# One buffer for both halves of a split weight, and matmul operands at whole multiples of 64 bytes from each other

## The chip, the cores and the metric

The kernel runs on one core of one Trainium2 chip. The metric is the device time of one execution in microseconds (us). Memory addresses below are byte offsets within a partition of the on-chip memory (SBUF), as the built programs have them.

## The reference

One layer of a decoder trunk, in float32, on x of 512 positions by 1024 channels:

```python
h = rms_norm(x, g_pre_mix)
z = h @ w_in                    # columns: u, v, q, six k/v, gates, xr, rg, mg
y_a = gmlp_mixer(gelu(u), gelu(v), ...)     # causal 128-position chunks
y_b = nsa_mixer(q, k.., v.., nsa_g, ...)    # 16 heads: compressed, selected, window
y_c = rglru_mixer(xr, rg, ...)  # conv of width 4, gates r and i by x @ w_a, x @ w_x, linear scan
gates = sigmoid(mg)             # one for each branch
merged = gates[0] * (y_a @ w_br_a) + gates[1] * (y_b @ w_br_b) + gates[2] * (y_c @ w_br_c)
x = x + rms_norm(merged @ w_o, g_post_mix)
f_gate, f_up = split(rms_norm(x, g_pre_ffn) @ w_ffn_in)
return x + rms_norm((silu(f_gate) * f_up) @ w_ffn_out, g_post_ffn)
```

## The kernel before

Every large product is done in three matmuls. A weight tile of 128 x 1024 comes in as `raw`; ACT writes its rounded high half `hi` (L119) and DVE the rest, `lo` = raw - hi (L124), both 128 x 1024. The activations are split the same way (`hh` and `hl` are the halves of the normalized input). `passes` (L236) then runs, for each of eight 128-row pieces of the contraction, hi times xh, hi times xl and lo times xh, each a matmul of 128 x 128 weights with 512 columns: 24 matmuls for one unit. Of each matmul the weights are the stationary operand, which is loaded while the matmul before still streams its moving operand.

The stages, in order: the v half of the projection (L538, to about 50 us); units of L236 with the recurrent branch between them (L464: six matmuls a piece, with the block weights `wabh`, `wabl` as stationary and the halves `ch`, `cl` of the convolved tile as moving operand); attention from 383 to 648 us, where units of L236 alternate with scores (L850), transposes (L875) and values (L888: `ph`, `pl` moving, `V` stationary); the output projection (L1067); the first layer of the feed-forward part in 256-column matmuls (L1169, and L1303 on pairs of weight tiles combined as in Strassen's scheme, where `a22h` and `a22l` are one of the combined operands); its second layer (L1439, 512 columns). L766 is the other 256-column stage, at 350 us.

The order of work around this is written as generators that yield between matmuls; a scheduler in the build places the instructions of each engine by what they wait for and by when a pool gives its buffer. `unit` (L231) takes the next weight and has three loaded ahead. Tiles live in pools; a pool's tiles lie behind one another at fixed addresses, so a pool's start follows from the sizes of the pools before it: `const`, `mid` (rows, and the small attention statistics `pcst` and `ast`), `stage` (raw), `merge`, `wts` (hi and lo, three buffers each), `big`, then one pool per phase. `warm` is a constant of one column, 4 bytes, at the start.

The distance spoken of below is the address of a matmul's moving operand minus that of the stationary operand of the next matmul. Weight and activation pieces are 512 and 2048 bytes long, so within one pair of tiles the distance modulo 512 is the same for all pieces.

Of the kernel before, what the change touches and what calls it, by code (L numbers as in the profile page):

```python
# [22 lines left out]
F32 = mybir.dt.float32  # L23
F32R = mybir.dt.float32r
# [26 lines left out]
def hybrid_block(ctx: ExitStack, tc: tile.TileContext, A, out):  # L51
# [3 lines left out]
    const = ctx.enter_context(tc.tile_pool(name="const", bufs=1))  # L55

    mid = ctx.enter_context(tc.tile_pool(name="mid", bufs=1))
    stage = ctx.enter_context(tc.tile_pool(name="stage", bufs=2))
    merge = ctx.enter_context(tc.tile_pool(name="merge", bufs=1))
    wts = ctx.enter_context(tc.tile_pool(name="wts", bufs=2))  # L60
# [17 lines left out]
    def next_phase(i):  # L78
        if phase[0]:
            phase[0].__exit__(None, None, None)  # L80
        if i == 2:
            early.__exit__(None, None, None)
        phase[0] = tc.tile_pool(name=f"phase{i}", bufs=1, reuse_waits="tile")
        pool = phase[0].__enter__()
        for t in PHASES[i]:
            phase_pool[t] = (pool, PHASES[i][t])

    phase_pool = {}

    cnt = [0]  # L90

    def nm(s):
        cnt[0] += 1
        return f"{s}_{cnt[0]}"
# [4 lines left out]

    def row(name, dt=F32, tag="row"):  # L100
        return mid.tile([128, S], dt, tag=tag, name=nm(name), bufs={"row": 6, "q32": 2, "tg": 2}[tag])

    def bank(tag):
        return psum[1].tile([128, S], F32, tag=tag, name=nm(tag), bufs=psum[2][tag])
# [78 lines left out]
    def wload(upto):  # L183
        while wnext[0] < min(upto, wlimit[0]):
            i = wnext[0]
            ap, tag = wlist[i]
            if isinstance(ap, tuple):
                hi = wts.tile([128, 1024], F32R, tag="hi", name=nm("hi"), bufs=3)
                lo = wts.tile([128, 1024], F32R, tag="lo", name=nm("lo"), bufs=3)
                fo["prep"](*ap, hi, lo)  # L190
                wready[i] = (hi, lo)
                wnext[0] += 1
                continue
            raw = stage.tile([128, 1024], F32, tag="raw", name=nm("raw"), bufs=2)
            parts = [slice(0, 512), slice(512, 1024)] if i == 0 else [slice(0, 1024)]
            for n, p in enumerate(parts):
                (SC if i == n == 0 else SY).dma_start(raw[:, p], ap[:, p])
                if i == 0:
                    x_in(n + 1)
            if tag == "gate":  # L200

                hi = lo = wts.tile([128, 1024], F32R, tag="hi", name=nm("hi"), bufs=3)
                SC.activation(hi, raw, AF.Copy)
                r, h = (t.rearrange("p (k m) -> p k m", m=128)[:, :, 64:] for t in (raw, hi))
                V.tensor_sub(h, r, f32(h))
                wready[i] = (hi, lo)
                wnext[0] += 1
                continue
            if tag:
                u = slab("u", F32R, tag, (2, 1024))  # L210
                hi, lo = u[:, 0], u[:, 1]
            else:
                hi = wts.tile([128, 1024], F32R, tag="hi", name=nm("hi"), bufs=3)
                lo = wts.tile([128, 1024], F32R, tag="lo", name=nm("lo"), bufs=3)
            todo = [(raw[:, p], hi[:, p], lo[:, p], V) for p in parts]
            if i == 0:
                wfirst.extend(todo)
            else:
                split(*todo[0])
            wready[i] = (hi, lo)  # L220
            wnext[0] += 1
# [33 lines left out]
    def x_in(k):  # L255
        SY.dma_start(xt[k], A["xT"][:, k, :])
# [4 lines left out]
    wload(1)  # L261
    ones = const0([128, 128], "ones")
    V.memset(ones, 1.0)
    warm = const.tile([128, 1], F32, name="warm")
    V.memset(warm, 0.0)
    SC.activation(warm, warm, AF.Exp)
    ident = const.tile([128, 128], F32, name="ident")
# [58 lines left out]
    hh, hl = Pair("hh", F32R, "h"), Pair("hl", F32R, "h")  # L326
# [454 lines left out]
    def cmp_attn(g):  # L781
        if g == 0:
            yb["y"] = Pair("yb", tag="yb")
        ps = bank("tr")
        pv = ps.rearrange("p (a h n) -> p a h n", a=4, h=4)
        for a in range(4):
            for p in range(2):
                PE.matmul(ps[:, a * 128 + p * 64:a * 128 + p * 64 + 64],  # L788
                          at[g]["q32"][p][:, a * 128:(a + 1) * 128], kcb[:, g, :], start=True, stop=True)
        P = row("pc").rearrange("p (a h n) -> p a h n", a=4, h=4)  # L790
        P3 = P.rearrange("p a h n -> p (a h) n")
        st = mid.tile([128, 2, 4, 4], F32, tag="pcst", name=nm("pcst"), bufs=2)
        s0 = st[:, 0].rearrange("p a h -> p (a h)")
        for h in range(4):
            V.scalar_tensor_tensor(P[:, :, h, :], pv[:, :, h, :], 0.125, cmask, op0=OP.mult, op1=OP.add)
        yield
        V.tensor_reduce(s0, P3, axis=mybir.AxisListType.X, op=OP.max)
        V.tensor_tensor(P3, P3, s0[:, :, None].to_broadcast([128, 16, 32]), op=OP.subtract)
        Pf = P.rearrange("p a h n -> p (a h n)")
        SC.activation(Pf, Pf, AF.Exp)  # L800
        yield
        V.tensor_reduce(s0, P3, axis=mybir.AxisListType.X, op=OP.add)
        V.reciprocal(s0, s0)
        V.tensor_mul(st[:, 0], st[:, 0], gates[:, :, 12 * g:12 * g + 12:3])
        V.tensor_mul(P3, P3, s0[:, :, None].to_broadcast([128, 16, 32]))
        yield
        pt = bank("tr")
        for a in range(4):
            PE.transpose(pt[:, a * 128:(a + 1) * 128], P[:, a].rearrange("p h n -> p (h n)"), ident)

        PT = [row("pct", F32R) for _ in range(2)]
        for p in range(2):
            own, other = slice(64 * p, 64 * p + 64), slice(64 - 64 * p, 128 - 64 * p)
            SC.activation(PT[p][own], pt[own], AF.Copy)
            V.tensor_sub(PT[p][other], pt[own], f32(PT[p][own]))
        yield
        gs = slice(128 * g, 128 * g + 128)
        for p in range(2):
            po = bank("tr")
            PE.matmul(po, vch[:, gs], PT[p], start=True, stop=False)  # L820
            PE.matmul(po, vcl[:, gs], PT[p], start=False, stop=True)
            SC.activation(yb["y"][2 * g + p], po, AF.Copy)
            yield

    class Unit:
# [14 lines left out]
        def scores(self, j):  # L840
            g, a, n, brs = self.g, self.a, self.n, self.brs
            w = len(brs)
            if j == 0:
                self.T = slab("P", tag="P")
                self.st = mid.tile([128, 3, 4, w], F32, tag="ast", name=nm("ast"), bufs=3)
            st, K = self.st, at[g]["k"]
            ps = bank("sc")
            lhs = at[g]["q"][:, j, a * 128:(a + 1) * 128]
            for i in range(2):
                PE.matmul(ps[:, :w * n].rearrange("p (b n) -> p b n", b=w), lhs, K[:, i, brs[0]:brs[-1] + 1, :n],  # L850
                          start=(i == 0), stop=(i == 1))
            for b, br in enumerate(brs):
                t = self.part(j, br)
                V.tensor_tensor_reduce(out=t, in0=ps[:, b * n:b * n + n], in1=mask[0][:, S - n:], scale=-0.125,  # L854
                                       scalar=3.0e38, op0=OP.add, op1=OP.min, accum_out=st[:, 0, j, b:b + 1])
                SC.activation(t, t, AF.Exp, scale=-1.0, bias=st[:, 0, j, b:b + 1],  # L856
                              accum_out=st[:, 1, j, b:b + 1])
            if j == 3:
                V.reciprocal(st[:, 2], st[:, 1])
                for b, br in enumerate(brs):  # L860
                    V.tensor_mul(st[:, 2, :, b], st[:, 2, :, b], gates[:, a, 12 * g + 1 + br:12 * g + 12:3])

                own = 0 if w == 2 else 2
                for i in range(own):
                    t = self.part(i, brs[0])
                    SC.activation(t, t, AF.Copy, scale=st[:, 2, i, 0:1])
                for b, br in enumerate(brs):
                    o = b * n
                    t = self.T[:, own:4, o:o + n]
                    V.tensor_tensor(t, t, st[:, 2, own:4, b:b + 1].to_broadcast([128, 4 - own, n]), op=OP.mult)  # L870
# [333 lines left out]
    def first_weights():  # L1204

        ff["raw"] = [slab("rawp", tag="w2", shape=(2, 1024))]
        pair_load(HEAD)
        for _ in range(9):
            yield
        w = [tuple(wts.tile([128, 1024], F32R, tag=t, name=nm(t), bufs=3) for t in ("hi", "lo")) for _ in range(3)]  # L1210
        ff["ring"] = w
        ff["prep"] = pair_prep(HEAD)
        for _ in range(4):
            next(ff["prep"])
            yield
# [514 lines left out]
```

## Time and profile before

| what | value |
|---|---|
| median of 3 runs | 1115.99 us (1115.6 to 1116.36) |
| profiled execution | 1115.29 us, its span 1113.6 us |
| granted TensorE clock, mean | 0.998 |
| TensorE (PE) busy | 1103.9 us, 99%, 6152 matmuls |
| weight loads (PEld) busy | 954.8 us, 86% |
| DVE, ACT, POOL busy | 827.7, 625.7, 46.2 us |
| read from DRAM | 111.89 MB, 102 GB/s over the span |

The profiled execution is 0.7 us under the median. In the profile's rows "L236 PE MATMUL mm<-hl,hi" names the line, the output, and behind the arrow the moving and the stationary operand; "idle before" is the time in which the engine stood still ahead of such instructions, and the arrow behind it names what ended it. A matmul's duration reaches from its start to its modelled end and overlaps the next one's; the distance of two starts is what it costs in a row of matmuls.

### The profile page before, as it was taken

The numbers are of one execution on the slowest core, as the hardware profiler recorded it, in microseconds if no ns is written. First come the engines' busy times: TensorE is split into PE (matmuls) and PEld (weight loads), VectorE is DVE, ScalarE is ACT, GpSimd is POOL, SyncE is SP. The second block draws the span as 40 slices with busy tenths as digits, with TensorE's granted clock in tenths as the row PEclk, the third lists the DMA queues.
The fourth block names the chain that finished last, engine by engine and source line by source line (L and its number), as shares of the span: only waits on it lengthen the run. The fifth ranks groups of instructions, "written<-read, shape, count | busy, mean of one in ns | idle before, by whom it ended". The sixth has DMA issues, their size and how long they took to land.

```text
span 1113.6 us, 15969 instructions
## 1 busy us (share of the span) xinstructions
PE 1103.9 (99%) x6152; PEld 954.8 (86%) x6152; DVE 827.7 (74%) x1453; ACT 625.7 (56%) x1120; POOL 46.2 (4%) x59
## 2 busy tenths in 40 slices
PE   9999999999999999999999999999999999999997
PEld 8888778888888888888878888888999999998885
DVE  6966967262575899998998853567988787879665
ACT  6756674232344676776776632435655655567552
POOL 1000202100000000000000000000000000022200
PEclk9999999999999999999999999999999999999999
DMA  8332325323222211112112163421233332378902
GB/s 310 114 95 76 103 93 192 108 89 98 90 81 77 77 58 38 57 30 79 45 40 75 54 230 95 129 99 38 77 114 115 114 107 84 133 192 218 186 29 94
DMA packets 34653, 115.02 MB, mean 103 GB/s; under 512 B 3409, under 2 KB 3697, under 8 KB 33425
## 3 DMA queue, kind: packets, MB, share of 16 engines
q1 hardware_dynamic: 27200, 93.78, 25.5%
q0 software_dynamic: 5216, 11.18, 5.1%
q10 hardware_dynamic: 2160, 9.04, 2.2%
q8 instruction: 48, 0.79, 0.3%
q14 instruction: 29, 0.23, 0.1%
HBM read 111.89 MB, written 2.10 MB: 102 GB/s over the span
## 4 chain that ended last, share of the span: by engine, by line
PE 92%; DVE 4%; ACT 2%; DMA 1%; issue 0%; DVEq 0%; ACTq 0%
PE mm L236 39%; PE mm L1303 18%; PE mm L1439 6%; PE mm L538 4%; PE mm L1067 4%; PE o L888 4%; PE sc L850 3%; PE tr L875 3%; PE tr L1439 3%; PE mm L766 2%; PE tr L682 1%; DVE lo L124 1%; PE mm L1169 1%; PE tr L464 1%; PE tr L598 1%; PE tr L788 1%
## 5 line engine op out<-in xcount | busy, mean ns | idle before, releaser
L119 ACT ACTIVATE hi<-raw 128x1024 fp32r<-128x1024 f32 (+1 forms) x108 | 113.4, 1050 | 156.0 <-PE mm L236 77.1
L236 PE MATMUL mm<-hh,hi 128*128 128x512 f32 x504 | 199.9, 397 | 0.0
L236 PE MATMUL mm<-hh,lo 128*128 128x512 f32 x504 | 197.5, 392 | 0.2 <-DVE lo L124 0.2
L236 PE MATMUL mm<-hl,hi 128*128 128x512 f32 x504 | 197.2, 391 | 0.0
L124 DVE TENSOR_TENSOR lo<-raw,hi 128x1024 fp32r<-128x1024 f32 (+1 forms) x108 | 131.6, 1219 | 80.1 <-ACT hi L119 73.0
L236 PEld LDWEIGHTS mm<-hh,lo 128*128 128x128 f32 x504 | 94.7, 188 | 20.1 <-DVE lo L124 0.5
L236 PEld LDWEIGHTS mm<-hh,hi 128*128 128x128 f32 x504 | 94.7, 188 | 18.7 <-ACT hi L119 0.4
L236 PEld LDWEIGHTS mm<-hl,hi 128*128 128x128 f32 x504 | 94.8, 188 | 18.5 <-issue 0.2
L856 ACT ACTIVATE P<-P,ast 128x128 f32<-128x128 f32 (+3 forms) x128 | 70.6, 554 | 23.2 <-DVE ast L854 22.6
L854 DVE CUSTOM_DVE_ANT_0 P<-sc,mask 128x128 f32<-128x128 f32 (+3 forms) x128 | 57.9, 484 | 8.2 <-PE sc L850 7.3
L119 ACT ACTIVATE ph<-tr 128x512 fp32r<-128x512 f32 x80 | 46.9, 591 | 29.3 <-PE tr L875 28.4
L124 DVE TENSOR_TENSOR pl<-tr,ph 128x512 fp32r<-128x512 f32 x80 | 54.4, 685 | 5.0 <-ACT ph L119 3.0
L1303 PE MATMUL mm<-t,hi 128*128 128x256 f32 x288 | 53.3, 283 | 0.0
L1390 POOL DMA_DIRECT2D bs<-in_w_fo x16 | 19.3, 1212 | 792.0 <-DVE lo L124 792.0
L850 PE MATMUL sc<-K,q 128*128 128x512 f32 (+2 forms) x192 | 50.9, 367 | 0.0
L1439 PE MATMUL mm<-hi,u 128*128 128x512 f32 x160 | 50.3, 390 | 0.0
L875 PE MATMUL tr<-ident,P 128*128 128x128 f32 x320 | 48.7, 273 | 0.0
L875 PEld LDWEIGHTS tr<-ident,P 128*128 128x128 f32 x320 | 39.1, 140 | 9.8 <-DVE pl L124 0.9
L124 DVE TENSOR_TENSOR lo<-bs,hi 128x1024 fp32r<-128x1024 f32 x28 | 34.1, 1221 | 14.6 <-ACT hi L119 14.6
L1303 PEld LDWEIGHTS mm<-t,hi 128*128 128x128 f32 x288 | 44.8, 192 | 0.0
L1303 PE MATMUL mm<-fh,hi 128*128 128x256 f32 x144 | 41.0, 285 | 0.0
L1303 PE MATMUL mm<-fh,lo 128*128 128x256 f32 x144 | 40.7, 283 | 0.0
(384 smaller groups left out, 2760.0 us busy)
## 6 DMA issues: line engine op xcount, KB each, us to landing
raw<-in_w_in SPq DMA_DIRECT2D x64, 512.0 KB, 3.6
rawp<-in_w_fi SPq DMA_DIRECT2D x20, 1024.0 KB, 4.9
raw<-in_w_br SPq DMA_DIRECT2D x24, 512.0 KB, 3.6
bs<-in_w_fo POOLq DMA_DIRECT2D x20, 512.0 KB, 6.8
w<-in_cw ACTq DMA_DIRECT2D x4, 1024.0 KB, 6.2
raw<-in_w_o SPq DMA_DIRECT2D x8, 512.0 KB, 3.6
bs<-in_w_fo SPq DMA_DIRECT2D x8, 512.0 KB, 7.4
raw<-in_w_v SPq DMA_DIRECT2D x7, 512.0 KB, 5.2
```

Of the source, the lines that this page charges most:

```text
L119: res["hi"] = SC.activation(hi, src, AF.Copy)
L124: res["lo"] = V.tensor_sub(lo, src, f32(hi))
L236: res["mm"] = PE.matmul(ps[:m, n0:n1], w[:, k * 128:k * 128 + m], x[k][:, n0:n1], start=(t == 0), stop=(t == 3 * NK - 1))
L538: res["mm"] = PE.matmul(b[c], x[k][:, c * 128:(c + 1) * 128], w[:, kk * 512:kk * 512 + 512], start=(k == 0 and t == 0), stop=(k == NK - 1 ...
L850: PE.matmul(ps[:, :w * n].rearrange("p (b n) -> p b n", b=w), lhs, K[:, i, brs[0]:brs[-1] + 1, :n], start=(i == 0), stop=(i == 1))
L854: V.tensor_tensor_reduce(out=t, in0=ps[:, b * n:b * n + n], in1=mask[0][:, S - n:], scale=-0.125, scalar=3.0e38, op0=OP.add, op1=OP.min, a ...
L856: SC.activation(t, t, AF.Exp, scale=-1.0, bias=st[:, 0, j, b:b + 1], accum_out=st[:, 1, j, b:b + 1])
L875: PE.transpose(pt[:, j * 128:(j + 1) * 128], self.part(j, br)[:, kt * 128:(kt + 1) * 128], ident)
L888: PE.matmul(po, VV[:, kt, g % 2, br].rearrange("p i d -> p (i d)"), x, start=(br == 0 and kt == 0 and t == 0), stop=(br == 1 and kt == a a ...
L1067: res["mm"] = PE.matmul(b[c, f], x[k][:, q], w[:, fs], start=(k == 0 and t == 0), stop=(k == NK - 1 and t == 2))
L1303: res["mm"] = PE.matmul(ps, w[:, k * 128:k * 128 + 128], x[:, k], start=(start and k == t == 0), stop=(k == 3 and t == 2), skip_group_chec ...
L1439: PE.matmul(ps, a, b, start=id(ps) not in begun, stop=i == len(ops) - 1, skip_group_check=True)
```

## The change

A function `wpair` gives both halves of a weight as two slices of one tile of 2080 columns with three buffers. In every second tile the halves begin 16 columns (64 bytes) later. The column halves of the gate unit take the first slice of such a tile. The small statistics `pcst` and `ast` move from the pool `mid` to the phase's pool, `warm` becomes 17 columns long (64 bytes more), and the third phase's pool begins with an unused tile of 256 bytes, `gap`. In names after, `hl` stands for such a weight tile too (as in `mm<-hh,hl`), whichever half is used.

```diff
+        if i == 2:
+            pool.tile([128, 64], F32, name="gap", bufs=1)
...
+    wturn = [0]
...
+    def wpair():
+        o = 16 * (wturn[0] % 2)
+        wturn[0] += 1
+        w = wts.tile([128, 2080], F32R, tag="hl", name=nm("hl"), bufs=3)
+        return w[:, o:o + 1024], w[:, o + 1024:o + 2048]
...
-                hi = wts.tile([128, 1024], F32R, tag="hi", name=nm("hi"), bufs=3)
-                lo = wts.tile([128, 1024], F32R, tag="lo", name=nm("lo"), bufs=3)
+                hi, lo = wpair()
...
-                hi = lo = wts.tile([128, 1024], F32R, tag="hi", name=nm("hi"), bufs=3)
+                hi = lo = wpair()[0]
...
-    warm = const.tile([128, 1], F32, name="warm")
+    warm = const.tile([128, 17], F32, name="warm")[:, 0:1]
...
-        st = mid.tile([128, 2, 4, 4], F32, tag="pcst", name=nm("pcst"), bufs=2)
+        st = phase_pool["q"][0].tile([128, 2, 4, 4], F32, tag="pcst", name=nm("pcst"), bufs=2)
...
-                self.st = mid.tile([128, 3, 4, w], F32, tag="ast", name=nm("ast"), bufs=3)
+                self.st = phase_pool["q"][0].tile([128, 3, 4, w], F32, tag="ast", name=nm("ast"), bufs=3)
...
-        w = [tuple(wts.tile([128, 1024], F32R, tag=t, name=nm(t), bufs=3) for t in ("hi", "lo")) for _ in range(3)]
+        w = [wpair() for _ in range(3)]
```

What it makes of the addresses, modulo 512 bytes:

| tiles | before | after |
|---|---|---|
| rows (`ch`, `cl`, `ph`, `pl`, `a22h`, ...) | 192 | 256 |
| halves of the weights | 224 | 256, 384 or 0 for the three buffers, and 64 more in every second tile |
| `h` and `y` slabs (`hh`, `hl`, ...) | 224 | 128 |
| attention's `q`, `K`, `V` | 224 | 128 |
| third phase's slabs (`mo`, `f`, ...) | 224 | 384 |
| first phase's `wabh`, `wabl` | 0 | 416 |

And of the distances, in numbers of matmuls by their columns:

| columns | distance modulo 512 | before | after |
|---|---|---|---|
| 512 | 0 | 3048 | 185 |
| 512 | 64, 128, ..., 448 | 37 | 3059 |
| 512 | no multiple of 64 | 227 | 68 |
| 256 | 0 | 1851 | 498 |
| 256 | 64, 128, ..., 448 | 0 | 1598 |
| 256 | no multiple of 64 | 245 | 0 |

No computing instruction is added or taken away. Some move: of TensorE's 6003 instructions about 180 stand at another place, of ACT's 984 about 90.

On TensorE the largest of these moves is in the second recurrent batch (130 to 160 us). `tr` are L464's outputs, `mm` those of a unit of L236, whose weight halves are `hi_1125` and `lo_1126`. Before:

```order
L236 MATMUL mm_1232<-hl_131,hi_1125 128x512
L464 MATMUL tr_1217<-ch_1171,wabh_526 128x512
L464 MATMUL tr_1226<-ch_1171,wabh_526 128x512
L236 MATMUL mm_1232<-hh_129,lo_1126 128x512
L236 MATMUL mm_1232<-hh_130,hi_1125 128x512
L236 MATMUL mm_1232<-hl_132,hi_1125 128x512
L464 MATMUL tr_1217<-cl_1172,wabh_526 128x512
L464 MATMUL tr_1217<-ch_1171,wabl_527 128x512
L464 MATMUL tr_1226<-cl_1172,wabh_526 128x512
L464 MATMUL tr_1226<-ch_1171,wabl_527 128x512
L236 MATMUL mm_1232<-hh_130,lo_1126 128x512
```

The same six after (L471 is L464 seven lines further down, L243 is L236):

```order
L243 MATMUL mm_1159<-hh_129,hl_1054 128x512
L471 MATMUL tr_1194<-ch_1149,wabh_516 128x512
L471 MATMUL tr_1203<-ch_1149,wabh_516 128x512
L243 MATMUL mm_1209<-hh_128,hl_1104 128x512
L471 MATMUL tr_1194<-cl_1150,wabh_516 128x512
L471 MATMUL tr_1194<-ch_1149,wabl_517 128x512
L471 MATMUL tr_1203<-cl_1150,wabh_516 128x512
L471 MATMUL tr_1203<-ch_1149,wabl_517 128x512
L243 MATMUL mm_1209<-hl_130,hl_1104 128x512
```

They stand now between two units, with one matmul of the next unit between the first two and the other four; before, they stood within a unit, with three of its matmuls between.

On ACT, in the first recurrent batch, the high copies of the weights (`hi`, after `hl`) and the convolved tiles' first steps (`xc`). Before:

```order
L119 ACTIVATE hi_634<-raw_632 128x1024
L119 ACTIVATE hi_674<-raw_672 128x1024
L454 ACTIVATE xc_662<-mm_631,vec 128x512
L119 ACTIVATE ch_667<-xc_662 128x512
L203 ACTIVATE hi_725<-raw_723 128x1024
L454 ACTIVATE xc_702<-mm_671,vec 128x512
```

After:

```order
L128 ACTIVATE hl_623<-raw_621 128x1024
L461 ACTIVATE xc_650<-mm_620,vec 128x512
L128 ACTIVATE hl_662<-raw_660 128x1024
L128 ACTIVATE ch_655<-xc_650 128x512
L461 ACTIVATE xc_689<-mm_659,vec 128x512
L211 ACTIVATE hl_712<-raw_710 128x1024
```

The second and the third copy stand one place later: behind the `xc` that they stood ahead of.

More of the change, by code (lines that the diff above doesn't have):

```diff
@@ L212, in wload @@
             else:
-                hi = wts.tile([128, 1024], F32R, tag="hi", name=nm("hi"), bufs=3)
-                lo = wts.tile([128, 1024], F32R, tag="lo", name=nm("lo"), bufs=3)
+                hi, lo = wpair()
             todo = [(raw[:, p], hi[:, p], lo[:, p], V) for p in parts]
```

## The prediction

> **What bounds the kernel now.** I read the page from the top, then the view of waits, the chain, and last the durations of single lines.
>
> ```profile
> PE 1103.9 (99%) x6152; PEld 954.8 (86%) x6152; DVE 827.7 (74%) x1453; ACT 625.7 (56%) x1120; POOL 46.2 (4%) x59
> ...
> PE 92%; DVE 4%; ACT 2%; DMA 1%; issue 0%; DVEq 0%; ACTq 0%
> PE mm L236 39%; PE mm L1303 18%; PE mm L1439 6%; PE mm L538 4%; PE mm L1067 4%; PE o L888 4%; PE sc L850 3%; PE tr L875 3%; PE tr L1439 3%; PE mm L766 2%; PE tr L682 1%; DVE lo L124 1%; PE mm L1169 1%; PE tr L464 1%; PE tr L598 1%; PE tr L788 1%
> ```
>
> TensorE is busy 99% of the span and makes 92% of the chain. The view of waits shows what it waited for:
>
> ```profile
> PE mm L321 <- DVE warm L265: 1.1, 1, 1.1
> PE tr L464 <- ACT ch L119: 0.7, 1, 0.7
> PE o L888 <- DVE yb L895: 0.4, 2, 0.2
> PE mm L236 <- DVE lo L124: 0.2, 1, 0.2
> ```
>
> The total is 2.4 us. No reordering or buffer change can win more than that; whatever the change is worth lies in the spacing from one matmul to the next. Unbroken pieces of the chain give it (start, length, line, count):
>
> ```profile
> 624 pieces in order of time: start us, us, what
> ...
> 74.51 1.39 PE tr L464 x6
> 75.90 5.49 PE mm L236 x24
> ...
> 235.72 53.09 PE mm L236 x234
> ...
> 350.51 11.51 PE mm L766 x96
> ...
> 390.16 0.93 PE o L888 x4
> ...
> 648.35 77.55 PE mm L236 x342
> ...
> 787.39 11.52 PE mm L1169 x96
> ...
> 1043.65 13.60 PE mm L1439 x60
> ```
>
> Length over count: a long run of 512-column matmuls takes 226.9, 226.8 and 226.7 ns for each (L236 twice, L1439). A long run of 256-column matmuls takes 119.9 and 120.0 (L766, L1169). The short pieces are dearer: L464 231.7, L888 232.5. The 24 matmuls of L236 directly behind L464 take 228.8, so a run that starts unsettled pays about 24 x 2.0 = 48 ns before it reaches its rhythm, and then keeps it for hundreds.
>
> The three kinds of piece differ in what the change touches: the distance between the moving operand of a matmul and the stationary operand that is loaded for the next one meanwhile (the table above). It is 0 modulo 512 bytes in the long runs, 192 in L464, and 32 off a multiple of 64 in L888 and in the a22 products of L1303. The lines' durations (minimum/median/maximum in ns) say the same:
>
> ```profile
> L236 PE MATMUL mm<-hh,hi x504: 387/389/791, 56.2 to 714.2; 128*128 128x512 f32 x168
> ...
> L464 PE MATMUL tr<-cl,wabh x16: 392/394/502, 67.8 to 148.8; 128*128 128x512 f32 x16
> L464 PE MATMUL tr<-ch,wabl x16: 392/393/398, 68.2 to 149.0; 128*128 128x512 f32 x16
> ...
> L888 PE MATMUL o<-ph,V x80: 389/397/510, 390.0 to 647.7; 128*128 128x512 f32 x80
> ...
> L1303 PE MATMUL mm<-fh,u x192: 283/283/283, 804.5 to 993.7; 128*128 128x256 f32 x192
> L1303 PE MATMUL mm<-t,a22h x160: 277/280/282, 807.4 to 999.4; 128*128 128x256 f32 x160
> ...
> L1303 PE MATMUL mm<-t,a22l x80: 278/281/283, 807.6 to 999.5; 128*128 128x256 f32 x80
> ```
>
> A duration holds the spacing and a fixed tail: 389 stands for 226.8 and 283 for 120, so the tail is 162 to 163. Then 280 stands for 117 and 277 for 114. The timeline confirms the first: the a22 products from the first of these rows to the start of the second are twelve in 1.41 us, 117.5 ns each.
>
> ```profile
> 867.62 0.40 PE L1303 MATMUL mm<-t,a22h 128*128 128x256 f32 x2
> ...
> 869.03 1.48 PE L1303 MATMUL mm<-t,u 128*128 128x256 f32 x11
> ```
>
> So distance matters, by a few ns, and in opposite senses: off zero the 256-column matmul is 2.5 to 3 ns cheaper than at zero, the 512-column one was never seen settled. That is the whole question. 1 ns on each of 3300 512-column matmuls is 3.3 us.
>
> **The change part by part.** *256-column matmuls.* The table has 1851 at distance zero before and 498 after: 1351 leave zero, and the others that stood off 64 now stand at whole multiples of it. Each of the 1351 gains between nothing and 6 ns (283 to the minimum 277). No 256-column row rises above 283 by its median, so I see no loss. By the a22 rows' median it is 3 ns, 4.1 us; by their minimum 8.1 us. Those rows are a half step (32) off; a whole step should separate the operands at least as well, so I take 4.5 ns, between median and minimum: -6.1 us, ends 0 and -8.1.
>
> *512-column matmuls.* How many are at stake outside attention (383 to 648 us), where runs are long: the L236 rows of the first and last window here, and then L538, L1067 and L1439 over the span.
>
> ```profile
> 0.00:383.00 383.00, 279.54 (x1189) 221.82 (x1190) 1.00 0.35 115
> ...
> 648.00:784.00 136.00, 89.63 (x438) 75.88 (x438) 1.00 0.38 126
> ```
>
> ```profile
> 0.00:1114.00 1114.00, 44.59 (x192) 36.01 (x192) 1.00 0.33 103
> ...
> 0.00:1114.00 1114.00, 44.78 (x192) 35.75 (x192) 1.00 0.33 103
> ...
> 0.00:1114.00 1114.00, 109.99 (x480) 89.74 (x480) 1.00 0.33 103
> ```
>
> 1189 + 438 + 192 + 192 + 480 = 2491, of which 3059 of 3312 (92%) stand off zero after: about 2300. Price of each: the lower end is the minimum of L236, 387, that is -2 ns and -4.6 us; the upper end is L464's 231.7 against 226.8, +4.9 ns and +11.3 us. I take 0. Nearest in distance is L464, and it speaks for the upper end; but its pieces are six matmuls long, and a run at distance zero is just as slow in its first matmuls (the 24 behind it at 228.8). A run of six cannot show whether its distance settles. That all long runs of both sizes end at one steady value, from whatever start, makes a steady value at other distances likelier than none, and 226.8 is the one seen.
>
> *Operands off 64.* Of the 512-column matmuls 227 stood off 64 and 68 do after; the 160 of L888 are most of the difference. At most 232.5 - 226.8 = 5.7 ns each, -0.9 us; but pieces of four will hardly settle, so -0.5, ends -0.9 and 0.
>
> *One ring instead of two, and the moved instructions.* A weight's high half could be overwritten one matmul before its low half; now both go together, and ACT's high copies stand one place later. These rows show the slack ahead of the copies (idle time, and what ended it):
>
> ```profile
> L119 ACT ACTIVATE hi<-raw 128x1024 fp32r<-128x1024 f32 (+1 forms) x108 | 113.4, 1050 | 156.0 <-PE mm L236 77.1
> ...
> L124 DVE TENSOR_TENSOR lo<-raw,hi 128x1024 fp32r<-128x1024 f32 (+1 forms) x108 | 131.6, 1219 | 80.1 <-ACT hi L119 73.0
> ```
>
> ACT waits 77 us for TensorE to free a buffer, while TensorE waits 0.2 us for a low half: a unit of 24 matmuls takes 24 x 0.2268 = 5.4 us, copy and subtraction 1.05 + 1.22 = 2.3 us, and two more units are loaded ahead. One matmul later (0.23 us) is covered by that. Were the cover gone, every unit's start would be 0.23 us late at most; over the 108 of this row 25 us, which I exclude, since three buffers remain. In the second recurrent batch a TensorE unit now ends between the wabh pairs instead of being cut by them; the low half `cl` is waited for on the same engine place. I take 0, ends -0.7 (the wait on `ch` gone) and +0.7 (one more like it). The tiles moved to the phase pool hold statistics that DVE and ACT use, and POOL, SP and the transfers do the same work as before: 0. The gap tile and the wider warm tile issue nothing.
>
> *Sum.* 1115.29 (the profiled execution) - 6.1 + 0 - 0.5 + 0 = 1108.7. The median of the runs is 0.7 above the profiled one, so 1109.4.
>
> **The rivals.** *The long 512-column runs lose their rhythm (slower).* The mechanism is that of L464: at 192 bytes the spacing is 231.7 and more, and it stays so. For it: no 512-column row off zero has a median under 393. Against it: all these pieces are short. Price: 2300 x 4.9 = +11.3, less 6.1: 1115.99 + 5.2 = 1121; with 256 columns at the median price 1123. It decides from (6.1 + 0.5) / 2300 = 2.9 ns on. At L888's 397, +8 ns, it would be about 1128.
>
> *Addresses don't matter and nothing happens.* Then the a22 rows are 3 ns cheaper for another reason, say that only their stationary and moving rows lie in other pools. For it: L236, L538, L1067 and L1439 run alike though their operands lie far apart. Against it: the a22 products stand in one accumulation with products at 283, in one line of code, and differ from them in the place of their operands. Time: 1115.3 to 1116.7. [...]
>
> *More comes free.* 512 columns cost 226.8 and 256 cost 119.9, so 256 further columns cost 106.9, and 119.9 - 106.9 = 13.0 ns is a fixed part of each matmul (an estimate from these rows). If whole steps of 64 bytes remove some of it from both sizes, then by the minima, 387 and 277: -4.6 - 8.1 - 0.9, 1102.4. If they removed all of it: (2300 + 1351) x 13.0 = 47 us, 1069. For it: the minima exist. Against it: they are single matmuls, and a22's 32 bytes took away 3 ns of 13. [...]
>
> **How the numbers follow.** Forecast (256-column cheaper, 512-column as before) 0.40, with its own range 1106 to 1112; lost rhythm 0.34; nothing 0.13; more free 0.13, of which 0.03 for the whole fixed part. Faster by over 0.2%: 0.53; within 0.2%: 0.13; slower: 0.34 (0.2%, 2.2 us, is about what a measurement of this kernel can tell from no change). The range goes from 1100, under the minima with 2 us for fewer unsettled starts, to 1126, the lost rhythm with 3 us of the way to L888's price. It leaves out some 0.05 below and 0.10 above.
>
> **What would show it.** Durations by line in the profile after. L1303's fh and t products at 277 to 280 where they were 283: the first term right; at 283: wrong. The long pieces of L236 in the chain at 226.8: second term right; at 231 to 232, median 393 or 394: the slower rival; at 224 to 225: more comes free. L888 under 394: third term. PE's waits above 3.1 us, or L124's low halves among them with more than 0.9: the ring costs something after all. Wrong altogether I would be if the spacing followed the distance modulo 512 finely, each multiple of 64 with its own price, since then the mean over 64 to 448 decides and none of my rows but one is such a distance.

## The result, and the profile after

The changed kernel takes 1121.68 us (median of 4 runs, 1120.9 to 1121.99) against 1115.8 before: a ratio of 1.0051, 95% interval 1.0034 to 1.0069. It is slower by 5.9 us. Forecast were 1109.4, with 0.34 on slower. The profiled execution has a span of 1119.7 us, 6.1 more than before, and the same granted clock, 0.998.

The view of TensorE's waits first (what waited, for what, us in total, times, longest):

```profile
PE mm L328 <- DVE warm L272: 1.1, 1, 1.1
PE o L895 <- DVE yb L902: 0.5, 2, 0.3
PE tr L471 <- ACT ch L128: 0.4, 1, 0.4
PE mm L545 <- ACT gxh L337: 0.3, 1, 0.3
PE mm L545 <- DVE vt L431: 0.2, 1, 0.2
```

They add up to 2.5 us, as against 2.4: the 6 us are in no wait. Now the chain's long pieces (L243 is L236 of before, L773 L766, L1074 L1067, L1310 L1303):

```profile
...
237.86 53.87 PE mm L243 x234
...
354.39 11.20 PE mm L773 x96
...
653.49 78.90 PE mm L243 x342
732.39 38.41 PE mm L1074 x168
...
805.73 193.96 PE mm L1310 x1644
```

The same counts as before: 234 matmuls went from 53.09 to 53.87 us (226.9 to 230.2 ns each), 342 from 77.55 to 78.90 (230.7). The 256-column pieces went the other way: 96 from 11.51 to 11.20 us, and L1310 against this piece of before:

```profile
798.91 196.52 PE mm L1303 x1644
```

119.5 ns became 118.0. The durations by line (minimum/median/maximum) show the same:

```profile
L243 PE MATMUL mm<-hh,hl x1008: 387/393/797, 57.7 to 720.9; 128*128 128x512 f32 x168
L243 PE MATMUL mm<-hl,hl x504: 387/393/481, 57.9 to 720.7; 128*128 128x512 f32 x168
...
L1310 PE MATMUL mm<-t,hl x432: 274/279/290, 805.6 to 989.5; 128*128 128x256 f32 x144
L1310 PE MATMUL mm<-fh,hl x288: 276/279/367, 790.3 to 996.5; 128*128 128x256 f32 x144
L1310 PE MATMUL mm<-t,u x288: 278/283/284, 812.7 to 999.4; 128*128 128x256 f32 x144
```

The first of these `t` rows stood before in two, with the high and the low halves as weights; the larger one was:

```profile
L1303 PE MATMUL mm<-t,hi x288: 280/283/283, 798.7 to 985.0; 128*128 128x256 f32 x144
```

389 became 393 and 283 became 279; 283 stays in the rows with `u` as weights: there nearly all steps stand at 0 or 256 (265 of the 288 of `t,u` at 256). Summed over every start-to-start step of the two traces, 3314 matmuls of 512 columns take 8.7 us more (771.0 to 779.7; L243 5.5, L1446 1.9, L545 1.2 of it), 2096 of 256 columns 2.8 us less (251.9 to 249.1), everything else together 0.3 more.

Sorted by the distance of the step, the steps of the trace after have a plain order. The spacing repeats in short patterns, and each belongs to a distance. In the table "steady" is what a run settles at, from this trace and those of e1 to e3 below:

| distance modulo 512 | 512 columns, steady, ns | 256 columns, steady, ns |
|---|---|---|
| 0, 256 | 226.7 (226, 227, 227 in turn) | 120 |
| 64, 320 | 229 (226, 229, 232 in turn) | 113.3 or 117.8 |
| 128, 384 | 232.6 (228 to 241 in a pattern of eight or nine) or 233.3 (229, 238 in turn) | 118.7 to 119.4 |
| 192, 448 | 233.3 (231, 236 in turn, or 233, 234) | 113.3 or 117.8 |

So 512-column matmuls lose at every distance but 0 and 256 (229 to 233.3 ns against 226.7), and 256-column ones gain most at the odd multiples of 64 (113.3 or 117.8 against 120). For 512 columns two distances that are 256 apart cost the same, so these rows would fit a rule modulo 256 as well as one modulo 512.

### The profile page after: what moved, and what is told of

Read it like the earlier page. It is cut to its first block, busy times and chain, and to the rows that moved or that the text cites. A ratio compares the mean times of both kernels' runs of the same rounds, so it can differ in the third digit from the quotient of the medians.

```text
span 1119.7 us, 15945 instructions
## 1 busy us (share of the span) xinstructions
PE 1109.8 (99%) x6152; PEld 951.8 (85%) x6152; DVE 827.2 (74%) x1453; ACT 624.5 (56%) x1120; POOL 46.5 (4%) x59
## 4 chain that ended last, share of the span: by engine, by line
PE 93%; DVE 2%; DMA 2%; ACT 1%; issue 0%; SPq 0%; DVEq 0%; ACTq 0%
PE mm L243 43%; PE mm L1310 18%; PE mm L1446 7%; PE mm L1074 4%; PE o L895 4%; PE sc L857 3%; PE tr L882 3%; PE tr L1446 3%; PE mm L773 2%; PE mm L545 2%; PE tr L689 1%; PE mm L1176 1%; PE tr L471 1%; DMA wabr<-in_wab 1%; DMA xrow<-in_x 1%; PE tr L605 1%
## 5 line engine op out<-in xcount | busy, mean ns | idle before, releaser
L243 PE MATMUL mm<-hh,hl 128*128 128x512 f32 x1008 | 333.0, 397 | 0.0
L243 PEld LDWEIGHTS mm<-hh,hl 128*128 128x128 f32 x1008 | 189.0, 188 | 40.8 <-DVE V L786 0.4
L243 PE MATMUL mm<-hl,hl 128*128 128x512 f32 x504 | 198.6, 394 | 0.0
L133 DVE TENSOR_TENSOR hl<-raw,hl 128x1024 fp32r<-128x1024 f32 (+1 forms) x108 | 131.2, 1215 | 69.4 <-ACT hl L128 69.2
L128 ACT ACTIVATE hl<-raw 128x1024 fp32r<-128x1024 f32 (+1 forms) x108 | 113.1, 1047 | 80.2 <-PE mm L243 34.1
L243 PEld LDWEIGHTS mm<-hl,hl 128*128 128x128 f32 x504 | 94.9, 188 | 19.7 <-issue 0.2
L1446 PE MATMUL mm<-hl,u 128*128 128x512 f32 x240 | 56.5, 394 | 0.0
L1310 PE MATMUL mm<-t,hl 128*128 128x256 f32 x432 | 56.2, 279 | 0.0
L1310 PE MATMUL mm<-fh,hl 128*128 128x256 f32 x288 | 56.0, 280 | 0.0
L1446 PEld LDWEIGHTS mm<-hl,u 128*128 128x128 f32 x240 | 44.9, 188 | 10.5 <-DVE u L133 0.2
L1310 PEld LDWEIGHTS mm<-t,hl 128*128 128x128 f32 x432 | 53.0, 188 | 0.0
L1310 PEld LDWEIGHTS mm<-fh,hl 128*128 128x128 f32 x288 | 46.3, 188 | 0.0
L243 PE MATMUL mm<-yah,hl 128*128 128x512 f32 x128 | 44.6, 398 | 0.0
```

Source lines behind the costliest of these rows:

```text
L128: res["hi"] = SC.activation(hi, src, AF.Copy)
L133: res["lo"] = V.tensor_sub(lo, src, f32(hi))
L243: res["mm"] = PE.matmul(ps[:m, n0:n1], w[:, k * 128:k * 128 + m], x[k][:, n0:n1], start=(t == 0), stop=(t == 3 * NK - 1))
L1310: res["mm"] = PE.matmul(ps, w[:, k * 128:k * 128 + 128], x[:, k], start=(start and k == t == 0), stop=(k == 3 and t == 2), skip_group_chec ...
L1446: PE.matmul(ps, a, b, start=id(ps) not in begun, stop=i == len(ops) - 1, skip_group_check=True)
```

## The experiments

Theory S: the spacing follows the distance modulo 512. Theory R: the ring and the order cost the time. Theory C: the changing of the distance from unit to unit costs it. The runs of before beside each set had medians of 1115.3 to 1115.4 us. The views shown are the chain's pieces, the durations by line and the timeline.

**e1, ring and alignment without the offsets.**

```diff
-        o = 16 * (wturn[0] % 2)
-        wturn[0] += 1
-        w = wts.tile([128, 2080], F32R, tag="hl", name=nm("hl"), bufs=3)
-        return w[:, o:o + 1024], w[:, o + 1024:o + 2048]
+        w = wts.tile([128, 2048], F32R, tag="hl", name=nm("hl"), bufs=3)
+        return w[:, :1024], w[:, 1024:]
...
-        if i == 2:
-            pool.tile([128, 64], F32, name="gap", bufs=1)
...
```

> One ring for both halves and every pool start at a multiple of 64 bytes as in the change, but without the offsets: weight tiles of 2048 columns, no 64 bytes more in every second one, no gap tile. All 2064 matmuls of 256 columns and 3119 of 512 columns then stand at distance 0. Theory S (the spacing of matmuls follows the distance modulo 512): 1115 us, 0.6 under before, from the few operands that stood 32 off; durations 389 in L236's line, 283 in L1303's, a22 too. Theory R (the ring and the moved instructions cost the 6 us): 1121. Theory C (what costs is that the distance changes from unit to unit, so that runs start unsettled): 1115 as well.

1115.52 us, ratio 1.000 (0.999 to 1.0009). The long run of L238 (L236 of before) is back at 226.9 ns:

```profile
234.69 53.09 PE mm L238 x234
```

The ring, the moved instructions, the moved statistics and the wider `warm` cost nothing that can be measured: R falls. The operands no longer 32 off gave nothing on balance: by the steps of the two traces the 256-column matmuls take 1.0 us more (251.9 to 252.9), as `a22` went from 117 back to 120 (median 283 where it was 280), and the 512-column ones 1.1 us less (771.0 to 769.9).

**e2, a constant distance of 256**, and **e3, of 192.** Each is e1 with an unused tile at the head of the pool `big`:

```diff
     big = ctx.enter_context(tc.tile_pool(name="big", bufs=1))
+    big.tile([128, 64], F32, name="pad", bufs=1)     # e2; 48 columns in e3
```

> As the first run of this set, with an unused tile of 256 bytes ahead of the slabs: 2840 matmuls of 512 columns and 1278 of 256 columns at a constant distance of 256. Theory S: the profile after shows 226.7 for 512 columns at 256 as at 0, and 120 for 256 columns, so 1115. A rival N (any distance but 0 keeps 512-column matmuls from their rhythm): 2840 x 4.9 = 14 us more, less 1278 x 3 = 4: 1126. Theory C: 1115.

> As the first run of this set, with 192 bytes ahead of the slabs: 2003 matmuls of 512 columns at a constant distance of 192, 837 at 320, 1100 of 256 columns at 192 and 178 at 320. Theory S, with the profile after's 233.3 (192), 229.0 (320) for 512 columns and 116 for 256 columns: about 14 us more and 6 less, 1122; L236's line at 395 to 397. Theory C: the distance is constant over hundreds of matmuls, so they settle at 226.7 and the 256-column gain stands alone, 1110.

e2: 1115.34 us, ratio 1.0001 (0.9992 to 1.0011). e3: 1124.57, ratio 1.0082 (1.0065 to 1.0099). The same pieces of L239 in e2,

```profile
234.73 53.09 PE mm L239 x234
```

and in e3:

```profile
238.43 54.61 PE mm L239 x234
...
656.09 79.80 PE mm L239 x342
```

226.9 ns at 256, 233.4 at 192, and 233.3 in a run of 342 that never leaves its pattern. That settles two rivals. Not every distance other than 0 hurts, since 256 does not. And a constant distance is no cure: 192, constant over hundreds of matmuls, is as dear as any distance seen. C's 1110 is 14 us off. S gave 1122; of the 2.6 us that it fell short the 256-column runs make 2.3 (1278 x 1.8 ns). They settled at 117.8 here, not at the 116 assumed. In the timeline of e3 twelve matmuls go from the first row's start to the second's in 1.42 us:

```profile
855.89 1.58 PE L1306 MATMUL mm<-t,hl 128*128 128x256 f32 x12
857.31 0.40 PE L1306 MATMUL mm<-t,a22h 128*128 128x256 f32 x2
```

**e4, the distances with two rings.**

```diff
-        w = wts.tile([128, 2080], F32R, tag="hl", name=nm("hl"), bufs=3)
-        return w[:, o:o + 1024], w[:, o + 1024:o + 2048]
+        w = [wts.tile([128, 1040], F32R, tag=t, name=nm(t), bufs=3) for t in ("hi", "lo")]
+        return w[0][:, o:o + 1024], w[1][:, o:o + 1024]
...
-                hi = lo = wpair()[0]
+                hi = lo = wts.tile([128, 1040], F32R, tag="hi", name=nm("hi"), bufs=3)[:, :1024]
```

> The change with two rings again, hi and lo in buffers of 1040 columns each, the alternation, the warm tile, the gap and the moved statistics kept: the distances are spread over multiples of 64 as in the change, and the order is nearer to that of before. Theory S: 8 us more than before, 1123 to 1124 (the sum of the profile after's means by distance over this kernel's counts). Theory R: 1116.

1120.71 us, ratio 1.0047 (1.0032 to 1.0062), with L243 at 230.1:

```profile
237.68 53.84 PE mm L243 x234
```

The loss comes with the distances alone, without the one ring: S over R again. The size was missed by 3 us, and most of that lies in the expected sum: by this trace's own counts, the means of the profile after give about 1121.2, hardly less than the change's profiled 1121.4. Here hi and lo of a unit stand at different distances, so the distance changes inside a unit and a run of one or two seldom reaches its pattern. That made some distances cheaper (at 192 and at 128 a mean of 231.7 and 231.4 ns where the change had 233.2 and 233.1) and others dearer (at 256 and at 320 229.8 and 230.1 where it had 228.7 and 229.2); over their counts the four come to -1.4 and +1.3 us. So the changing of the distance has a price of its own at the cheaper distances, as C says, and a gain at the dearest. On balance it is no cost here, and it doesn't explain the 6 us.

**e5, the change without the 64 bytes in every second tile.**

```diff
-        o = 16 * (wturn[0] % 2)
+        o = 0
```

> The change with one line altered: the halves of every weight tile begin at column 0, so the 64 bytes in every second tile are gone; the tiles stay 2080 columns wide. 512-column matmuls: 999 at distance 128, 982 at 256, 980 at 384; 256-column: 640 at 0, 615 at 128, 479 at 256, 330 at 384. Theory S (each distance has its spacing, as the profiles so far show it: 226.7 at 0 and 256, 232.5 at 128 and 384, 119 to 120 for 256 columns at all four): 8 us over before, 1123.5, so 2 us slower than the change. Theory C (the changing of the distance costs): under the change, 1119 or less.

1122.84 us, ratio 1.0065 (1.005 to 1.008): C's 1119 or less is excluded, S's 1123.5 near. Against the change's own interval (1.0034 to 1.0069) the two overlap; whether the alternation helps by 1 us stays open.

**e6, only `t` at 320; e7, `t` and `y` at 320.** The tiles `t` of the feed-forward pairs start 80 columns later in buffers 128 columns longer (in `slab`); e7 puts 80 columns ahead of the `y` slabs and 48 between them and the `h` slabs.

```diff
+        if tag == "mo":
+            o = 80 if name == "t" else 0
+            w = pool.tile([128, 4 * S + 128], dt, tag=tag, name=nm(name), bufs=bufs)[:, o:o + 4 * S]
...
```

> The first of the variants (one ring, all at distance 0) with one family of tiles moved: the 256-column halves `t` of the feed-forward activations begin 320 bytes later in buffers of the third phase that are 512 bytes longer. 958 matmuls of 256 columns stand at 320, all others at 0. Two steady spacings were seen at odd multiples of 64: 113.3 in the change's profile and 117.8 at the constant distance of 192. Theory S with the change's mean at 320 (114.1): 1109. Theory E (which of the two a run takes follows from the distance of the run before; behind distance 0 it took 117.8 in all 44 runs at 192): 2.1 us under the variant at distance 0, 1113.

> As e6, and the `y` slabs 320 bytes further too: 1866 matmuls of 256 columns at a constant 320, and for it 584 of 512 columns at 320 and 285 at 192. Theory S with 114.1 for 256 columns: 1107. Theory E, one long run that enters from 512-column work and stays at 117.8: 1866 x 2.1 = 3.9 us less and 584 x 2.3 + 285 x 6.6 = 3.2 us more, 1114.5.

e6: 1113.70 us, ratio 0.9983 (0.9973 to 0.9992). e7: 1115.10, ratio 0.9997 (0.9987 to 1.0006). Both came as theory E had it: two steady spacings exist at one and the same distance (at 320 the change's profile has 113.3 ns), and behind distance 0 a run takes the slower. In e6 the twelve `t,u` matmuls take 1.41 us, 117.5 each:

```profile
839.21 1.57 PE L1310 MATMUL mm<-t,u 128*128 128x256 f32 x12
840.62 0.29 PE L1310 MATMUL mm<-fh,hl 128*128 128x256 f32 x1
```

**e8, `t` at 192 behind runs at 256.** As e6 with 48 columns in place of 80, and 64 columns each ahead of the `y` and of the `h` slabs.

> As e6, but `t` begins 192 bytes later and the `y` slabs stand at 256, so that the runs of twelve at 192 come from runs at 256, and 512-column matmuls stand only at 0 and 256. Theory E: behind 256 the four runs at 192 in the change's profile settled at 113.3 after five matmuls, mean 115.1: 958 x 4.8 = 4.6 us less and a few tenths from 256, 1110 to 1111. Without an effect of the entry (117.8 as in the constant run): 1113. 512-column matmuls as before in both.

1110.16 us, ratio 0.995 (0.9933 to 0.9966): the fastest of all. The same twelve matmuls take 1.36 us, 113.3 each:

```profile
838.34 1.52 PE L1313 MATMUL mm<-t,u 128*128 128x256 f32 x12
839.70 0.28 PE L1313 MATMUL mm<-fh,hl 128*128 128x256 f32 x1
```

Of 40 runs at 192 (12, 24 or more long) behind runs at 256 all 40 settled at 113.3 here; of 44 behind runs at distance 0 (40 in e3, four in the change's profile) all 44 at 117.7 to 117.9. One of the 40 was broken by a pause and shows both spacings at one distance. The twelve matmuls ahead of the pause settled at 113.3, the next one started 0.45 us behind the twelfth (0.18 us of idle time is put down to a wait for ACT), and the last twelve of the run took 117.5 ns each (946.20 to 947.61, 1.41 us):

```profile
942.96 1.54 PE L1313 MATMUL mm<-t,hl 128*128 128x256 f32 x12
944.68 0.50 PE L1313 MATMUL mm<-t,a22h 128*128 128x256 f32 x2 [0.18 <-ACT r L1371]
...
946.20 1.58 PE L1313 MATMUL mm<-t,hl 128*128 128x256 f32 x12
947.61 0.28 PE L1313 MATMUL mm<-fh,hl 128*128 128x256 f32 x1
```

The 41st run at 192, behind 512-column work at 0, took 117.8. The durations show `t` at 276, `fh` at 256 bytes still at 283, and the 512-column line untouched:

```profile
L246 PE MATMUL mm<-hh,hl x1008: 387/389/791, 57.7 to 715.2; 128*128 128x512 f32 x168
...
L1313 PE MATMUL mm<-t,hl x432: 276/276/286, 799.4 to 981.0; 128*128 128x256 f32 x144
L1313 PE MATMUL mm<-fh,hl x288: 278/283/364, 784.0 to 988.0; 128*128 128x256 f32 x144
```

**e9, all addresses moved by 192.**

```diff
-    warm = const.tile([128, 17], F32, name="warm")[:, 0:1]
+    warm = const.tile([128, 65], F32, name="warm")[:, 0:1]
```

> The variant at distance 0 (e1) with the constant `warm` 192 bytes longer, so that every tile behind it lies 192 bytes further and all distances stay 0. Theory S: as e1, 1115.5; L236's line at 389. Rival A (the address itself matters, not the distance): L236 at 391 or more, 4 us or more of difference.

1115.46 us, ratio 1.0003 (0.9994 to 1.0012), the piece of 234 at 53.09 again:

```profile
234.62 53.09 PE mm L238 x234
```

It is the distance, not the address: with 192 in the distances themselves (e3) the time was 1124.57.

**e10, `t` at 320 behind 256; e11, `t` at 192 with one of four at 256 and `y` at 320.** e10 is e8 with 80 columns for 48; e11 is e7 with these starts:

```diff
+            o = {"t": 48, "t4": 64}.get(name, 0)
...
-        t = {n: slab("t", F32R, "mo", (2, 4, 256)) for n in (1, 2, 3, 4)}
+        t = {n: slab("t4" if n == 4 else "t", F32R, "mo", (2, 4, 256)) for n in (1, 2, 3, 4)}
```

> As e8 with `t` at 320 bytes instead of 192, still behind runs at 256. Theory E: 320 behind 256 has not been seen; if 256 is what leads into the faster of the two spacings, 113.3 to 115, so 1110; if 320 behaves as behind distance 0 (e6), 117.8 and 1113.5.

> As e7 with three of the four `t` tiles at 192 and the fourth at 256, the `y` slabs at 320: in each round of 84 products of the pairs one run of twelve stands at 256, the others at 192 and 320. Theory E: the run at 256 leads into 113.3, and the runs at 320 and 192 behind it keep it, as 24 and 36 matmuls in a row at 192 did in e8: some 1430 x 6.4 = 9.1 us less, and 3.2 us more from 584 and 285 matmuls of 512 columns at 320 and 192, so 1108.5. If each change of distance loses it: 117.8, 1114.5.

e10: 1113.81 us, ratio 0.9988 (0.9979 to 0.9997). e11: 1112.86, ratio 0.9974 (0.9965 to 0.9984). In e10 all 40 runs at 320 took 117.6 to 117.9, behind 256 as behind 0, so 256 does not by itself lead to the faster spacing. In e11 the runs at 192 settled at 113.3 in 37 of 40 behind 320 and in all 19 behind 256, but those at 320 fell back to 117.8 in all 39, and the time lies between the two expected:

```profile
L1313 PE MATMUL mm<-t,hl x432: 276/276/286, 801.2 to 982.8; 128*128 128x256 f32 x144
L1313 PE MATMUL mm<-fh,hl x288: 279/279/365, 786.1 to 989.8; 128*128 128x256 f32 x144
```

Behind a longer run, which spacing a run takes goes with its distance and with that of the run before, the same in nearly every case (all 44, all 40, 37 of 40, all 19 and all 39 above); a rule for it was not found. Behind a single step one has to look further back. In the change's profile 320 behind a single step at 64 took 113.3 in all 8 cases, but 64 behind a single step at 320 took 113.3 in four cases, where that step followed a run at 0, and 117.8 in four others, where it followed a run at 128.

## Why the prediction was wrong

*What bounds the kernel* held: no wait changed by more than some tenths, and the whole difference is spacing. *The ring and the order at 0* held, by e1 and e4. (`unit`, put at L231 above, stands at L225.)

*512-column matmuls at 0* is the step that failed. It measured +8.7 us, near the upper end of +11.3. The reasoning was that all long runs end at one steady value from whatever start, so a run at another distance would end there too. But all those long runs stood at distance 0; they were evidence about 0 alone. The run of 342 in e3 shows that another distance has a steady value of its own, 233.3. The only row of before that stood at a nonzero multiple of 64, L464 at 231.7, did point the right way. I had discounted it because its runs are short, and a discount is a reason to widen, not to take the other end.

*256-column matmuls at -6.1* had the right sign and twice the size: -2.8 measured. The 4.5 ns per matmul were taken as one price for all distances. 128, 256 and 384, where 924 of the 1598 stand, give 0 to 1.4 ns; only the odd multiples give 2.2 or 6.7 once settled.

*Operands off 64 at -0.5*: nothing. The values' median durations moved by 2 ns at most and their time not at all (40.1 us before, 40.3 after, all 160 steps).

```profile
L895 PE MATMUL o<-ph,V x80: 390/395/503, 393.9 to 652.9; 128*128 128x512 f32 x80
L895 PE MATMUL o<-pl,V x80: 387/394/482, 394.1 to 653.1; 128*128 128x512 f32 x80
```

The slower rival came nearest: at every other distance but 256 the spacing is dearer and stays so, though in a pattern that is as steady as that at 0. It had 4.9 ns for all of 2300 matmuls and gave 1121. That this is within 1 us is luck: its 512-column term was 2.6 us too large and its 256-column gain 3.3 us, and the two errors cancel. Its turning point, 2.9 ns, used the gain that came out half as large; with -2.8 us it is 1.2 ns, and L243's two long pieces lost 3.3 and 3.9. The last sentence of the prediction named what happened, each multiple of 64 with its own price, and put no chance on it.

*Addresses don't matter* fell: e1 and e3 differ in 192 bytes of padding and in 9 us (1115.52 and 1124.57), and e9, at 1115.46, shows that the address alone is not it. There is a price that goes with the distance between moving operand and weights: in the piece of 234, 226.9 ns for each matmul at 0 (e1) and 233.4 at 192 (e3).

## What to carry to other kernels

Where TensorE is the bound and the matmul stream is long, compute for each stage the distance between the moving operand and the next weights modulo 512 bytes, and compare the spacing of long pieces of the chain, not of short ones. Here 0 and 256 were best for 512 columns (226.7 ns) and 192, behind runs at 256, for 256 columns (113.3), so one padding for all stages loses: 1124.57 us with 192 bytes (e3), 1115.34 with 256 (e2). Shift the tiles of one stage so that the others stay at 0 or 256, as e8 does (1110.16). A steady value seen at one setting need not hold at another (226.7 at 0, 233.3 at 192): without a run, keep the only row that has the new setting as the forecast, however short its pieces.

## What the runs showed of the hardware

Not expected was the regularity: spacing repeats in patterns of 1 to 9 matmuls that depend on the distance and persist for hundreds (341 steps at 192 in e3, mean 233.3). Nor was it expected that one distance has two steady spacings, 113.3 and 117.8 ns for 256 columns, chosen by what ran before: 44 of 44 runs at 192 behind distance 0 settled at the slower, 40 of 40 behind 256 at the faster, and behind a pause one of these went on at the slower (117.5). Whether the distance that counts is that to the next weights, which are loaded meanwhile (in the change's profile loads are busy for 951.8 us of the span of 1119.7, matmuls for 1109.8), or that to the weights already loaded, stays open, since within a run the two are the same. Where they differ the steps don't agree. In e3 the 256-column steps go with the next weights: 117.5 ns in 40 steps with the next at 192 and their own at 0, and 119.9 in 41 the other way round. In e4 the 512-column steps do the opposite: 229.5 ns in 110 steps with the next at 192 or 448 and their own at 0 or 256, and 234.3 in 107 the other way round. What makes the pattern was not measured.
